# The first stage of a one-core encoder kernel: other queues, another order of loads and units

## The chip, the core and the metric

The kernel runs on one NeuronCore of a Trainium2 chip. The time is the device time of one execution in microseconds (us), as a median of several; less is better. Beside TensorE (PE, matrix products), VectorE (DVE), ScalarE (ACT) and GpSimd (POOL) there is SyncE (SP), which here only issues DMAs. Each engine works its own queue in order.

## The reference, cut to what matters

Two layers over `x` (1024 tokens, width 1024) and a memory of 256 tokens. What the change touches is the beginning: the norms of `mem` and `x`, and the first products that use them.

```python
def rmsnorm(x, g):
    y = x * rsqrt(mean(x * x, axis=-1) + EPS)
    return y * g

mem_n = rmsnorm(mem, mem_norm)                 # 256 x 1024
k, v = split(mem_n @ w_mem_kv[l], 2)           # for both layers l
h = rmsnorm(x, norm_even[0])                   # 1024 x 1024
qA, kA, vA, gA, qB, zBf, zBb, iB, gB, qM, gM = split_cols(h @ w_in_even[0], EVEN_SIZES)
...                                            # attention and gated scans, layer 2, final norm
```

## The kernel before, in words

All products are in float32 precision made from three passes. `split_w` rounds a loaded weight tile `raw` to a high part `hi` (ScalarE, two copies of 128x512) and computes the rest `lo` (VectorE, two subtractions); `mm3` then issues the three matmuls high x high, high x low, low x high (L195 to L197) for each of 8 slices of the inner dimension. Loads go through `load`, which issues them on SyncE in the order of the program; raw tiles `wr` have 2 buffers, `hi` (`wh`) and `lo` (`wl`) have 3 each, PSUM tiles of products (`mm`) 2, of transposes (`so`) 2.

`norm_T` normalizes up to four tiles of 128 tokens and turns them: squares with row sums on ScalarE (L254), the inverse root on VectorE in nine tiny steps (`rsqrt`, L137 to L152), the scaling on VectorE (L258), then for each of 8 slices the transposes on TensorE (L262), the product with the norm's weights and rounding on ScalarE (L266, the high half) and the low half on VectorE (L267). The norm's weights are columns of `vec`, which `vectors()` makes: seven small loads into `vrow`, 16 warm-up matmuls on the identity (L81), one transpose (L83) and a copy to `vec` (L84).

The stage starts with `mem_norm_T`. Then `start` hands out units: products of the memory with `w_mem_kv` (four with K columns, `proj_fm`, and two with V columns, `proj_tm`, for layer 0), the loads of the two halves of `x` (`x_load`), the norms of these halves, and the value product `v` of the first pair of B heads (columns O_IB of `w_in_even`, eight tiles of 128 tokens, copied out by VectorE at L871). `constants()` computes masks (L105 to L118), the lower bound `lbt` (L92 to L98, with one Exp on ScalarE at L94) and the sink factors `sks` (L127, from the small load `skr`). `weave` runs a unit's load one unit ahead of its work.

The order on each engine is not that of the program: a scheduler that works at compile time takes instructions by priority and by its own estimate of when they are ready. Instructions under `tc.high_priority()` go first; loads under `keep_in_program_order` keep their order. What it decided can be read from the built program, engine by engine.

Of the kernel before, what the change touches and what calls it, by code (L numbers as in the profile page):

```python
# [13 lines left out]
ALU = mybir.AluOpType  # L14
# [10 lines left out]
WARM = 16  # L25
MASK = -1e30
# [11 lines left out]
def tile_kernel(ctx, tc, x, mem, norm_even, w_in_even, sink, lb_param, hgrn_norm, w_out_even,  # L38
# [34 lines left out]
    def vectors():  # L73
        vrow = st([NV, P], "t2")
        for off, src, n in ((V_MN, mem_norm, 8), (V_NE, norm_even[0], 8), (V_NO, norm_odd[0], 8),
                            (V_HN, hgrn_norm[0], 4), (V_GN, gla_norm[0], 8)):
            load(vrow[off:off + n, :], src.rearrange("(a p) -> a p", p=P))
        load(vrow[V_LB:V_LB + 8, :], lb_param[0].rearrange("d (a p) -> (d a) p", p=P))
        load(vrow[V_BG:V_BG + 8, :], b_gate[0].rearrange("d (a p) -> (d a) p", p=P))
# [80 lines left out]

    def split_w(raw, hi, lo):

        k = raw.shape[1] // 2
        for i in range(2):
            ks = slice(i * k, i * k + k)
            nc.scalar.copy(hi[:, ks], raw[:, ks])  # L166
            nc.vector.tensor_tensor(lo[:, ks], raw[:, ks], f32(hi[:, ks]), ALU.subtract)  # L167
# [13 lines left out]
    def load_tm(w, c0, n=256):  # L181

        r = []
        for kh in range(2):
            raw = st([P, KT // 2, n], "wr")
            load(raw, w[kh * 512:kh * 512 + 512, c0:c0 + n].rearrange("(k p) c -> p k c", p=P))
            hi, lo = st([P, KT // 2, n], "wh", F32R), st([P, KT // 2, n], "wl", F32R)
            split_w(raw, hi, lo)
            r.append((hi, lo))
        return r  # L190
# [36 lines left out]
    def proj_tm(w, c0, hT, cb, n=256, nt=NT):  # L227
# [13 lines left out]
        yield Unit(lambda: box.append(load_tm(w, c0, n)), lambda: run(0))  # L241
# [3 lines left out]
    def norm_T(tiles, gv, hh, hl):  # L245
# [9 lines left out]
        with tc.high_priority():  # L255
            y = rsqrt(ss[:, :n], n, 1.0 / D)
            for i, xt in enumerate(tiles):
                nc.vector.tensor_scalar(xn[i], xt, y[:, i:i + 1], None, ALU.mult)  # L258
        for k in range(KT):
# [5 lines left out]
            with tc.high_priority():  # L265
                nc.scalar.activation(hh[:, k, :], pv, AF.Identity, scale=g)  # L266
                nc.vector.scalar_tensor_tensor(hl[:, k, :], pv, g, f32(hh[:, k, :]), ALU.mult, ALU.subtract)  # L267
# [465 lines left out]
    def x_load():  # L733
# [64 lines left out]
    kv = chain(mem_kv(0, mT), mem_kv(1, mT))  # L798

    def start(v):  # L800
# [3 lines left out]

        yield from some(2)
# [62 lines left out]
    def even_main():  # L868
        for pair in range(2):
            Vt = st([P, NT, 256], "t8")  # L870
            v = proj_tm(W0, O_IB + 256 * pair, hT, lambda t, ps, Vt=Vt: nc.vector.tensor_copy(Vt[:, t, :], ps))  # L871
# [275 lines left out]
```

## Time and profile before

| | before |
|---|---|
| median of 3 runs | 1489.28 us (1489.16 to 1489.79) |
| profiled execution, its own time | 1488.72 us |
| its span in the trace | 1486.9 us |
| TensorE busy | 1455.1 us (98% of the span) |
| VectorE, ScalarE, GpSimd busy | 885.0, 679.6, 33.8 us |
| mean granted TensorE clock | 0.994 of full speed |

The span runs from the first to the last recorded instruction; the profiled execution lasted 1.8 us longer. Times below are us from the span's start. An engine's wait is shown in square brackets behind the instruction that ended it: how long it sat idle, and who released it. "x4" is a count of merged instructions. [...]

### The profile page before, as it was taken

What the parts mean: (1) busy time and instruction counts of PE and PEld (TensorE: products, weight loads), DVE (VectorE), ACT (ScalarE), POOL (GpSimd) and SP (SyncE); (2) the same over time, 40 slices, a digit from 0 to 9 for tenths busy, and PEclk for the clock granted to TensorE, in tenths of its full rate; (3) what the DMA queues carried; (4) which work ended last, traced back from release to release, by engine and by line L of the source; (5) the groups of instructions that cost most, each with busy time, mean ns of one, the idle gap of its engine ahead of it and who ended that gap; (6) DMA issues with size and microseconds to landing.
All of it is one profiled execution on the core that took longest, in us unless ns stands there. A gap on an engine that the chain in (4) does not pass through costs nothing.

```text
span 1486.9 us, 27605 instructions
## 1 busy us (share of the span) xinstructions
PE 1455.1 (98%) x11337; PEld 1209.0 (81%) x11337; DVE 885.0 (60%) x2112; ACT 679.6 (46%) x1497; POOL 33.8 (2%) x75
## 2 busy tenths in 40 slices
PE   7999999999999999999999999999999999999997
PEld 7888898889776777888788797979788888878885
DVE  6536767675786474535376458585653456652577
ACT  6434333443476465435246455454346433641353
POOL 0000000000000000000000000000001000000000
PEclk9999999999999999999999999999999999999998
DMA  7424111011100213111264111101113221101622
GB/s 226 158 85 145 56 30 44 30 30 44 34 25 36 71 43 121 43 29 29 92 240 142 43 46 28 33 26 34 40 41 123 79 87 43 30 15 43 238 88 100
DMA packets 104231, 107.39 MB, mean 72 GB/s; under 512 B 13012, under 2 KB 85768, under 8 KB 103592
## 3 DMA queue, kind: packets, MB, share of 16 engines
q1 hardware_dynamic: 97848, 86.15, 18.6%
q0 software_dynamic: 5104, 17.37, 3.0%
q8 instruction: 89, 1.46, 0.4%
q10 hardware_dynamic: 1152, 2.10, 0.4%
q14 instruction: 38, 0.31, 0.1%
HBM read 84.64 MB, written 20.97 MB: 71 GB/s over the span
## 4 chain that ended last, share of the span: by engine, by line
PE 84%; DVE 8%; ACT 6%; issue 1%; DMA 1%; SPq 0%; ACTq 0%
PE pmm L196 21%; PE pmm L195 21%; PE pmm L197 21%; PE pso L413 4%; DVE big L342 3%; ACT s L308 2%; PE pso L579 2%; PE plv L377 1%; PE pat L574 1%; PE plv L398 1%; DVE wl L167 1%; ACT wh L166 1%; PE pat L335 1%; PE pat L500 1%; PE pat L361 1%
## 5 line engine op out<-in xcount | busy, mean ns | idle before, releaser
L195 PE MATMUL pmm<-hT,wh 128*128 128x512 f32 x896 | 355.4, 397 | 1.6 <-ACT wh L166 1.5
L196 PE MATMUL pmm<-hT,wh 128*128 128x512 f32 x896 | 354.5, 396 | 0.0
L197 PE MATMUL pmm<-hT,wl 128*128 128x512 f32 x896 | 353.3, 394 | 0.0
L167 DVE TENSOR_TENSOR wl<-wr,wh 128x512 fp32r<-128x512 f32 x188 | 127.2, 688 | 183.9 <-ACT wh L166 173.4
L166 ACT CAST wh<-wr 128x512 fp32r<-128x512 f32 x188 | 113.6, 620 | 258.0 <-PE pmm L196 167.6
L195 PEld LDWEIGHTS pmm<-hT,wh 128*128 128x128 f32 x896 | 168.3, 188 | 36.0 <-ACT wh L166 2.2
L197 PEld LDWEIGHTS pmm<-hT,wl 128*128 128x128 f32 x896 | 168.3, 188 | 34.8 <-issue 0.8
L196 PEld LDWEIGHTS pmm<-hT,wh 128*128 128x128 f32 x896 | 168.4, 188 | 33.3 <-issue 0.4
L195 PE MATMUL pmm<-wh,hT 128*128 128x256 f32 x448 | 128.5, 287 | 0.0
L197 PE MATMUL pmm<-wh,hT 128*128 128x256 f32 x448 | 127.4, 284 | 0.0
L196 PE MATMUL pmm<-wl,hT 128*128 128x256 f32 x448 | 127.3, 284 | 0.0
L602 DVE TENSOR_TENSOR ms<-big,ms 128x256 fp32r<-128x256 f32 x192 | 80.4, 422 | 62.5 <-ACT ms L601 59.7
L601 ACT CAST ms<-big 128x256 fp32r<-128x256 f32 x192 | 77.3, 406 | 85.8 <-PE pmm L197 72.1
L196 PE MATMUL pmm<-hT,ms 128*128 128x512 f32 x256 | 100.4, 392 | 0.4 <-DVE hT L167 0.4
L195 PE MATMUL pmm<-hT,ms 128*128 128x512 f32 x256 | 100.1, 391 | 0.0
L197 PE MATMUL pmm<-hT,ms 128*128 128x512 f32 x256 | 99.9, 390 | 0.0
L195 PEld LDWEIGHTS pmm<-wh,hT 128*128 128x128 f32 x448 | 86.3, 193 | 0.1
L196 PEld LDWEIGHTS pmm<-wl,hT 128*128 128x128 f32 x448 | 86.3, 193 | 0.1
L197 PEld LDWEIGHTS pmm<-wh,hT 128*128 128x128 f32 x448 | 86.3, 193 | 0.0
L308 ACT COPY s<-big 128x1024 f32<-128x1024 f32 x40 | 47.1, 1177 | 66.8 <-DVE big L342 63.1
L749 DVE TENSOR_TENSOR big<-big,t 128x512 f32<-128x512 f32 x48 | 33.0, 689 | 71.1 <-ACT t L747 71.0
L342 DVE TENSOR_TENSOR big<-big,tsm 128x512 f32<-128x512 f32 x96 | 61.1, 688 | 14.1 <-ACT s L308 7.0
(257 smaller groups left out, 2588.0 us busy)
## 6 DMA issues: line engine op xcount, KB each, us to landing
wr<-in_w_in_even_dram SPq DMA_DIRECT2D x34, 512.0 KB, 3.5
wr<-in_w_in_odd_dram SPq DMA_DIRECT2D x32, 512.0 KB, 4.1
wr<-in_w_mem_kv_dram SPq DMA_DIRECT2D x16, 512.0 KB, 5.3
x<-xi POOLq DMA_DIRECT2D x32, 256.0 KB, 2.3
t<-x SPq DMA_DIRECT2D x16, 512.0 KB, 4.9
wr<-in_w_out_odd_dram SPq DMA_DIRECT2D x12, 512.0 KB, 4.4
kv<-s POOLq DMA_DIRECT2D x8, 512.0 KB, 4.4
i<-in_x_dram SPq DMA_DIRECT2D x8, 512.0 KB, 7.7
```

Of the source, the lines that this page charges most:

```text
L166: nc.scalar.copy(hi[:, ks], raw[:, ks])
L167: nc.vector.tensor_tensor(lo[:, ks], raw[:, ks], f32(hi[:, ks]), ALU.subtract)
L195: nc.tensor.matmul(ps, ah, bh, start=(i == 0), stop=False)
L196: nc.tensor.matmul(ps, ah, bl, start=False, stop=False)
L197: nc.tensor.matmul(ps, al, bh, start=False, stop=(i == last))
L308: nc.scalar.copy(kh.rearrange("p (b h j) -> p b h j", h=2, j=m), sub(Xa, 0, [[2 * m, nb], [3 * N + m, 2], [1, m]]))
L342: nc.vector.tensor_tensor(xv, xv, tv, ALU.mult)
L413: nc.tensor.matmul(po[:, :dv], a, b, start=(j == 0), stop=(j == len(ops) - 1))
L579: nc.tensor.matmul(po[64 * i:64 * i + 64, :], va[:, b0 + b - 1, ks], PT[b - 1][:, 256 * i:256 * i + 256], start=(b == 1), stop=(b == nb))
L601: nc.scalar.copy(ms[:, 0], src)
L602: nc.vector.tensor_tensor(ms[:, 1], src, f32(ms[:, 0]), ALU.subtract)
L749: nc.vector.tensor_tensor(ds, ds, tmp, ALU.mult)
```

## The change

Five things, all in the first 80 us of the program:

- `vectors()` is called before the loads of `mem`; its seven small loads go to GpSimd's queue; `vec` is copied by ScalarE with high priority; five more identity matmuls (`KEEP`) stand behind the transpose.
- The first weight's rounding is queued behind that copy and behind the scaling of `mem` (`issue_after` keeps an instruction behind a named one of the same engine), the second's behind the fourth slice of the mem norm.
- `x` comes in quarters of two tiles, and the units that load them stand earlier.
- The value weights of the first pair are loaded early in four quarters into tiles that are idle there (`ms`, `xi`), and rounded from these (new lines L198 and L199).
- The two V products of the memory no longer stand between the loads and norms of `x`: both norms and the value product come before them.

```diff
@@ vectors()
-            load(vrow[off:off + n, :], src.rearrange("(a p) -> a p", p=P))
+            nc.gpsimd.dma_start(vrow[off:off + n, :], src.rearrange("(a p) -> a p", p=P))
...
         nc.tensor.transpose(vps, vrow, ident[:NV, :NV])
-        nc.vector.tensor_copy(vec, vps)
+        with tc.high_priority():
+            behind.append(nc.scalar.copy(vec, vps).ins)
+        for _ in range(KEEP):
+            nc.tensor.matmul(pt("mm")[:, :P], ident, ident, start=True, stop=True)
@@ split_w
+        with ExitStack() as order:
+            for i in behind.pop(0) if behind else ():
+                order.enter_context(tc.issue_after(i))
+            for i in range(2):
...
@@ load_tm(w, c0, n=256, raws=None)
+            if raws:
+                for i in range(2):
+                    ks = slice(2 * i, 2 * i + 2)
+                    nc.scalar.copy(hi[:, ks], raws[2 * kh + i])
+                    nc.vector.tensor_tensor(lo[:, ks], raws[2 * kh + i], f32(hi[:, ks]), ALU.subtract)
@@ mem_norm_T
+        vectors()
         tiles = []
...
-        vectors()
         mT = st([P, 2, KT, NMEM], "big", F32R)
-        norm_T(tiles, V_MN, mT[:, 0], mT[:, 1])
+        scaled, moved = norm_T(tiles, V_MN, mT[:, 0], mT[:, 1])
+        behind.append([behind.pop(), scaled])
+        behind.append(moved[3])
@@ x_load
-            if t % 4 == 3:
-                yield tiles[t - 3:]
+            if t % 4 % 2 == 1:
+                yield tiles[t - t % 4:]
@@ load_early (new)
+        for i in range(4):
+            raw = st([P, 2, 256], "ms" if i < 3 else "xi")
+            load(raw, W0[256 * i:256 * i + 256, O_IB:O_IB + 256].rearrange("(k p) c -> p k c", p=P))
+            yield raw
@@ start
         yield from some(2)
-        yield then(lambda: xh.append(next(xl)))
-        yield from some(2)
-        yield then(lambda: norm_T(xh[0], V_NE, *hT[0]))
+        yield x_part()
         yield from some(1)
-        yield then(lambda: xh.append(next(xl)))
+        yield x_part()
+        yield from some(1)
+        yield Unit(lambda: raws.extend(load_early()), lambda: None)
+        yield x_part()
+        yield x_part()
+        yield then(lambda: norm_T(xh[1], V_NE, *hT[0]))
         yield next(v)
-        yield then(lambda: norm_T(xh[1], V_NE, *hT[1]))
-        yield from some(1)
+        yield then(lambda: norm_T(xh[3], V_NE, *hT[1]))
         yield then(constants)
```

The order that the scheduler makes of it is shown at three places. In names, `t` in a norm is the scaled tile, `pso` the PSUM tile of a transpose, `pmm` that of a product, `big_149` and `big_159` the normalized memory, `hT` the normalized x. A line of the changed kernel is 9 to 33 higher than the same line before.

ScalarE, from the second square of `mem` on, before:

```order
L254 ACTIVATE t_38_151,sm_150<-i_16_102 128x1024
L254 ACTIVATE t_38_151,sm_150<-i_17_104 128x1024
L166 CAST wh_221<-wr_219 128x512 x2
L166 CAST wh_229<-wr_227 128x512 x2
L266 ACTIVATE big_149<-pso_166,vec 128x256
L266 ACTIVATE big_149<-pso_171,vec 128x256
L94 ACTIVATE lbt<-lbt 128x8
```

and in the changed kernel:

```order
L269 ACTIVATE t_43_161,sm_160<-i_39_155 128x1024
L269 ACTIVATE t_43_161,sm_160<-i_40_157 128x1024
L86 COPY vec<-pso_142 128x52
L175 CAST wh_231<-wr_229 128x512 x2
L98 ACTIVATE lbt<-lbt 128x8
L282 ACTIVATE big_159<-pso_176,vec 128x256
L282 ACTIVATE big_159<-pso_181,vec 128x256
L282 ACTIVATE big_159<-pso_186,vec 128x256
```

The copy of `vec` is now here and the first rounding behind it; the Exp of `lbt` (L94, now L98) has moved ahead of the first high half (L266, now L282), and the second weight's rounding behind the first high halves.

VectorE, ahead of the first low half of the memory, before:

```order
L167 TENSOR_TENSOR wl_222<-wr_219,wh_221 128x512 x2
L114 TENSOR_TENSOR mask_78<-mask_78,mi 128x32
L127 TENSOR_SCALAR sks<-skr 128x1 x2
L167 TENSOR_TENSOR wl_230<-wr_227,wh_229 128x512 x2
L84 COPY vec<-pso_146 128x52
L92 TENSOR_TENSOR lbt<-vec 128x8
L93 TENSOR_TENSOR lbt<-vec,lbt 128x8
L267 SCALAR_TENSOR_TENSOR big_149<-pso_166,vec,big_149 128x256
```

and in the changed kernel, from the last mask on:

```order
L118 TENSOR_TENSOR mask_78<-mask_78,mi 128x32
L131 TENSOR_SCALAR sks<-skr 128x1 x5
L96 TENSOR_TENSOR lbt<-vec 128x8
L131 TENSOR_SCALAR sks<-skr 128x1 x2
L97 TENSOR_TENSOR lbt<-vec,lbt 128x8
L131 TENSOR_SCALAR sks<-skr 128x1
L176 TENSOR_TENSOR wl_232<-wr_229,wh_231 128x512 x2
L283 SCALAR_TENSOR_TENSOR big_159<-pso_176,vec,big_159 128x256
L283 SCALAR_TENSOR_TENSOR big_159<-pso_181,vec,big_159 128x256
```

Between the scaling of `mem` and these rows stand 14 more mask instructions, which before stood partly between the steps of `rsqrt`. One weight's low part (L167, now L176) instead of two stands ahead of the first low half, and the copy of `vec` is gone.

TensorE, where the transposes of the second half of `x` begin, before:

```order
L196 MATMUL pmm_613<-wl_522,hT_83 128x256
L197 MATMUL pmm_613<-wh_521,hT_84 128x256
L262 MATMUL pso_676<-ident,t_111_656 128x128
L262 MATMUL pso_683<-ident,t_111_656 128x128
L262 MATMUL pso_676<-ident,t_111_656 128x128
L262 MATMUL pso_683<-ident,t_111_656 128x128
L195 MATMUL pmm_732<-wh_641,big_149 128x256
L196 MATMUL pmm_732<-wl_642,big_149 128x256
L197 MATMUL pmm_732<-wh_641,big_149 128x256
L195 MATMUL pmm_732<-wh_641,big_149 128x256
```

and in the changed kernel:

```order
L211 MATMUL pmm_557<-wl_397,hT_83 128x256
L212 MATMUL pmm_557<-wh_396,hT_84 128x256
L278 MATMUL pso_604<-ident,t_104_584 128x128
L278 MATMUL pso_611<-ident,t_104_584 128x128
L278 MATMUL pso_604<-ident,t_104_584 128x128
L278 MATMUL pso_611<-ident,t_104_584 128x128
L278 MATMUL pso_604<-ident,t_105_587 128x128
L278 MATMUL pso_611<-ident,t_105_587 128x128
L278 MATMUL pso_604<-ident,t_105_587 128x128
L278 MATMUL pso_611<-ident,t_105_587 128x128
L210 MATMUL pmm_717<-wh_390,hT_85 128x256
L211 MATMUL pmm_717<-wl_391,hT_85 128x256
```

Before, the V products of the memory (`pmm_732`) stand between the transposes; now the eight first transposes follow each other directly behind the fourth value tile (`pmm_557`), and the next products need the result of these transposes. The transposes of the first half read alike: between them stood `pmm_457`, and now nothing stands there.

## Rows read from the trace of the kernel before

**Rows 1.** Timeline, VectorE, first 24 us: start, duration, engine, line, operation, count, wait.

```profile
6.86 0.17 DVE L137 TENSOR_SCALAR sm<-sm 128x2 f32<-128x2 f32 x1 [6.86 <-ACT t L254]
...
8.80 1.41 DVE L258 TENSOR_SCALAR t<-i,sm 128x1024 f32<-128x1024 f32 x2
...
10.31 0.15 DVE L127 TENSOR_SCALAR sks<-skr 128x1 f32<-128x1 f32 x1
10.38 0.17 DVE L112 TENSOR_SCALAR mi<-mi 128x32 int32<-128x32 int32 x1
...
10.59 0.19 DVE L114 TENSOR_TENSOR mask<-mask,mi 128x32 int32<-128x32 int32 x1
...
12.40 1.28 DVE L167 TENSOR_TENSOR wl<-wr,wh 128x512 fp32r<-128x512 f32 x2
13.60 0.21 DVE L84 COPY vec<-pso 128x52 f32<-128x52 f32 x1
...
14.41 0.48 DVE L267 SCALAR_TENSOR_TENSOR big<-pso,vec,big 128x256 fp32r<-128x256 f32 x1 [0.21 <-ACT big L266]
...
21.56 0.88 DVE L267 SCALAR_TENSOR_TENSOR big<-pso,vec,big 128x256 fp32r<-128x256 f32 x2 [0.92 <-ACT big L266]
```

**Rows 2.** Timeline, ScalarE, 13 to 25 us.

```profile
13.90 0.47 ACT L266 ACTIVATE big<-pso,vec 128x256 fp32r<-128x256 f32 x1 [1.97 <-DVE vec L84]
...
23.38 1.06 ACT L254 ACTIVATE t<-big 128x1024 f32<-128x1024 f32 x1
```

**Rows 3.** Timeline, TensorE, start of the third product with the memory.

```profile
24.00 0.38 PE L195 MATMUL pmm<-big,wh 128*128 128x256 f32 x1 [0.45 <-DVE s L457]
```

**Rows 4.** Timeline, VectorE, scaling of the first half of x.

```profile
28.88 2.07 DVE L258 TENSOR_SCALAR t<-big,sm 128x1024 f32<-128x1024 f32 x3
...
31.20 0.74 DVE L258 TENSOR_SCALAR t<-big,sm 128x1024 f32<-128x1024 f32 x1
```

**Rows 5.** Chain of waits, 24 to 43 us: start, duration, what.

```profile
33.17 6.73 DMA wr<-in_w_in_even_dram
```

**Rows 6.** Timeline, ScalarE, rounding of the first layer's value weights.

```profile
40.00 0.62 ACT L166 CAST wh<-wr 128x512 fp32r<-128x512 f32 x1 [3.88 <-DMA wr<-in_w_in_even_dram]
```

**Rows 7.** Timeline, TensorE, last matmul before the gap, transposes behind it.

```profile
38.86 0.28 PE L197 MATMUL pmm<-wh,hT 128*128 128x256 f32 x1
42.06 1.10 PE L262 MATMUL pso<-ident,t 128*128 128x128 f32 x4 [2.92 <-DVE hT L267]
```

**Rows 8.** Windows: busy us and instructions by engine, PEclk, DMA share, GB/s.

```profile
11.00:11.50 0.50, 0.00 (x0) 0.00 (x0) 0.50 (x2) 0.50 (x2) 0.00 (x0) 0.90 0.00 0
...
42.00:42.50 0.50, 0.44 (x2) 0.44 (x3) 0.17 (x2) 0.50 (x2) 0.00 (x0) 0.62 1.08 412
45.50:46.00 0.50, 0.50 (x6) 0.50 (x5) 0.46 (x1) 0.50 (x1) 0.00 (x0) 0.97 1.00 324
```

**Rows 9.** Timeline, ScalarE, high halves of the second half of x.

```profile
57.88 1.27 ACT L266 ACTIVATE hT<-pso,vec 128x512 fp32r<-128x512 f32 x2 [7.51 <-PE pso L262]
...
66.03 0.69 ACT L266 ACTIVATE hT<-pso,vec 128x512 fp32r<-128x512 f32 x1 [0.26 <-PE pso L262]
```

**Rows 10.** Timeline, TensorE, end of the value product.

```profile
77.82 0.28 PE L197 MATMUL pmm<-wh,hT 128*128 128x256 f32 x1
77.94 0.28 PE L195 MATMUL pmm<-big,wh 128*128 128x256 f32 x1
```

**Rows 11.** Timeline, GpSimd, DMA issues.

```profile
31.57 0.54 POOL L469 DMA_DIRECT2D kv<-s  x1 [0.30 <-DVE s L457]
...
777.03 0.99 POOL L976 DMA_DIRECT2D wr<-in_w_gate_up_dram  x2 [0.29 <-POOL wr L974]
```

**Rows 12.** DMA issues by kind: count, KB each, us to landing.

```profile
wr<-in_w_gate_up_dram POOLq DMA_DIRECT2D x2, 32.0 KB, 1.9
skr<-in_sink_dram POOLq DMA_DIRECT2D x1, 4.0 KB, 4.5
```

**Rows 13.** Window of 200 us, columns as in rows 8.

```profile
350.00:550.00 200.00, 194.47 (x1496) 149.14 (x1495) 130.23 (x376) 114.25 (x289) 10.97 (x20) 1.00 0.13 43
```

More of the change, by code (lines that the diff above doesn't have):

```diff
@@ L25 @@
 WARM = 16
+KEEP = 5
 MASK = -1e30
@@ L76, in vectors @@
                             (V_HN, hgrn_norm[0], 4), (V_GN, gla_norm[0], 8)):
-            load(vrow[off:off + n, :], src.rearrange("(a p) -> a p", p=P))
-        load(vrow[V_LB:V_LB + 8, :], lb_param[0].rearrange("d (a p) -> (d a) p", p=P))
-        load(vrow[V_BG:V_BG + 8, :], b_gate[0].rearrange("d (a p) -> (d a) p", p=P))
+            nc.gpsimd.dma_start(vrow[off:off + n, :], src.rearrange("(a p) -> a p", p=P))
+        nc.gpsimd.dma_start(vrow[V_LB:V_LB + 8, :], lb_param[0].rearrange("d (a p) -> (d a) p", p=P))
+        nc.gpsimd.dma_start(vrow[V_BG:V_BG + 8, :], b_gate[0].rearrange("d (a p) -> (d a) p", p=P))
         for _ in range(WARM):
@@ L159, in half @@
         return slice(th * 512, th * 512 + 512)
+    behind = []
     def split_w(raw, hi, lo):
         k = raw.shape[1] // 2
[L164 to L167, printed above, removed]
+        with ExitStack() as order:
+            for i in behind.pop(0) if behind else ():
+                order.enter_context(tc.issue_after(i))
+            for i in range(2):
+                ks = slice(i * k, i * k + k)
+                nc.scalar.copy(hi[:, ks], raw[:, ks])
+                nc.vector.tensor_tensor(lo[:, ks], raw[:, ks], f32(hi[:, ks]), ALU.subtract)
     def load_fm(w, cols):
@@ L179, in load_fm, with load_tm @@
         return hi, lo, n
-    def load_tm(w, c0, n=256):
+    def load_tm(w, c0, n=256, raws=None):
         r = []
         for kh in range(2):
-            raw = st([P, KT // 2, n], "wr")
-            load(raw, w[kh * 512:kh * 512 + 512, c0:c0 + n].rearrange("(k p) c -> p k c", p=P))
             hi, lo = st([P, KT // 2, n], "wh", F32R), st([P, KT // 2, n], "wl", F32R)
-            split_w(raw, hi, lo)
+            if raws:
[3 more added lines that the diff above has]
+                    nc.vector.tensor_tensor(lo[:, ks], raws[2 * kh + i], f32(hi[:, ks]), ALU.subtract)
+            else:
+                raw = st([P, KT // 2, n], "wr")
+                load(raw, w[kh * 512:kh * 512 + 512, c0:c0 + n].rearrange("(k p) c -> p k c", p=P))
+                split_w(raw, hi, lo)
             r.append((hi, lo))
@@ L240, in run @@
                     cb(t, ps)
-        yield Unit(lambda: box.append(load_tm(w, c0, n)), lambda: run(0))
+        yield Unit(lambda: box.append(load_tm(w, c0, n, raws)), lambda: run(0))
         if nt > 4:
@@ L257, in norm_T @@
             for i, xt in enumerate(tiles):
-                nc.vector.tensor_scalar(xn[i], xt, y[:, i:i + 1], None, ALU.mult)
+                scaled = nc.vector.tensor_scalar(xn[i], xt, y[:, i:i + 1], None, ALU.mult)
+        done = []
         for k in range(KT):
@@ L265, in norm_T @@
             with tc.high_priority():
-                nc.scalar.activation(hh[:, k, :], pv, AF.Identity, scale=g)
-                nc.vector.scalar_tensor_tensor(hl[:, k, :], pv, g, f32(hh[:, k, :]), ALU.mult, ALU.subtract)
+                a = nc.scalar.activation(hh[:, k, :], pv, AF.Identity, scale=g)
+                d = nc.vector.scalar_tensor_tensor(hl[:, k, :], pv, g, f32(hh[:, k, :]), ALU.mult, ALU.subtract)
+                done.append((a.ins, d.ins))
+        return scaled.ins, done
     def new_hT(l):
@@ L803, in some, with x_part @@
             return (next(kv) for _ in range(n))
+        def x_part():
+            return Unit(lambda: xh.append(next(xl)), lambda: None)
         yield from some(2)
-        yield then(lambda: xh.append(next(xl)))
-        yield from some(2)
-        yield then(lambda: norm_T(xh[0], V_NE, *hT[0]))
+        yield x_part()
         yield from some(1)
-        yield then(lambda: xh.append(next(xl)))
+        yield x_part()
[4 more added lines that the diff above has]
+        yield then(lambda: norm_T(xh[1], V_NE, *hT[0]))
         yield next(v)
-        yield then(lambda: norm_T(xh[1], V_NE, *hT[1]))
-        yield from some(1)
+        yield then(lambda: norm_T(xh[3], V_NE, *hT[1]))
         yield then(constants)
```

7 lines of the change are left out of this document (5 added, 2 removed).

## Prediction

> **What bounds the kernel now.** I read the page's busy times first, then windows, then the timeline of each engine up to 80 us and the chain of waits from 24 to 43. TensorE is busy for 98% of the span, and behind the first stage it hardly stops: the worst 200 us, from 350 to 550, leave it idle for 200 - 194.47 = 5.5 us [rows 13]. So the change has to win in the first stage. That stage ends at 77.94, where the eight value tiles are done and the next product begins [rows 10]. By the order TensorE has then run 384 matmuls of 256 columns and 80 transposes; two matmuls start 0.12 apart [rows 10] and a transpose takes about as long, so 464 x 0.12 = 55.7 us of work, and 22.2 us are lost. The reader should see three losses. The first high half of the mem norm starts at 13.90, released by the copy of `vec` [rows 2], which stands behind two pairs of weight roundings [rows 1]. TensorE idles 2.92 us until 42.06 [rows 7], because ScalarE waited 3.88 us for the value weights [rows 6], a load under way for 6.73 us [rows 5]. And TensorE's granted clock fell to its lower level (1.2 GHz) twice, near 11.45 and near 42.1, after stretches with nothing or a few transposes; the second time it was back at 45.5 [rows 8]. These 3.4 us at half speed cost 1.7 us of work.
>
> **The head.** GpSimd issues two small loads in 0.99 us [rows 11], so seven from about 1.0, with the identity between, end near 5, and land 1.9 to 4.5 us after their issue [rows 12]: `vec` is there between 7.6 (the end of the warm-up) and 9.5. That is far earlier than 13.60 [rows 1], but the next thing in line is late too. On ScalarE the Exp of `lbt` now stands ahead of the first high half, and it waits for VectorE, where 15 mask rows and the sink factors come first. The norm's inverse root ends as before; without masks between its steps the scaling ends at 10.1 instead of 8.80 + 1.41 = 10.2 [rows 1]. A row that needs its predecessor follows it after 0.21 (10.38 to 10.59), a free one after 0.07 (10.31 to 10.38) [rows 1]. Nine mask rows wait for VectorE itself by the order: 9 x 0.21 + 6 x 0.07 = 2.3, then five sink factors 0.35, then two steps of `lbt` 0.4: 13.1, the Exp 0.2: the first high half at 13.3, 0.6 earlier. Bounds: all 23 rows free, 11.7; all dependent, 14.9. VectorE still has one weight's low part ahead of the first low half, 1.28 [rows 1]: 13.1 + 1.3 = 14.4, against 14.41 [rows 1]. The third slice's transposes wait for that half (two buffers), so nothing is won there. Stepping through the other slices by these durations, with TensorE at its upper clock, the last low half ends at 21.7 instead of 21.56 + 0.88 = 22.4, and the third product starts at 23.45 instead of 24.00 [rows 3]: **-0.55** (0 if the clock falls here as before, -2 if the rows are all free). The five extra matmuls run in idle time, up to 9.7; only if `vec` came after 11.3 would the weight's rounding, and with it the stage, be later.
>
> **Fourth product.** Its weight's low part stands on VectorE behind seven steps of x's inverse root, which wait for the last square of x. Two copies of K results are now ahead of that square, so it ends at 25.05 instead of 23.38 + 1.06 + 0.2 = 24.6 [rows 2]; 25.05 + 7 x 0.2 + 0.7 = 27.15, and TensorE, ready at 26.45, idles **+0.7** (0 to 1.2). It ends at 29.8.
>
> **First half of x.** The scaling ends at 32.05, as before (31.20 + 0.74 [rows 4]), since VectorE was the bound already. But the V product of the memory, 48 matmuls or 5.8 us, lay beside it and now stands far behind. From 29.8 until the first high half is ready at 33.25 TensorE has eight transposes, 1.0 us: **+2.5** (1.5 to 3.2).
>
> **Value weights.** Their quarters need no `wr` buffer; they are issued at 19 to 20, right behind the fourth K weight, and wanted at 26.6. Even the slow load took 6.73 [rows 5], so they are there. The idle 2.92 and the slow clock behind it go: **-4.6** (2.92 + 1.7; -2.9 if that clock fall comes elsewhere). The loads of x's second half land around 31, ten us before use, which hides them; a delay beyond 41 would count in full.
>
> **Second half of x.** Each slice takes about 1.2: the last six of the old second half came at (66.03 - 58.5)/6 = 1.26, with weight roundings between [rows 9]. So the first two value tiles, woven with the slices, end at 42.2, the next two at 42.55 + 48 x 0.12 = 48.3. The four squares stand behind the last high half on ScalarE: 41.0 + 4 x 1.06 = 45.2. VectorE copies the third tile, takes nine steps (1.8), four scalings at 0.67 (2.07 for three [rows 4]) and a copy: 50.85, and the first high half is ready at 52.05. Before, three value tiles and a V product lay beside this chain; now only two value tiles, and TensorE idles from 48.3 to 52.05 less 1.0 of transposes: **+2.8** (2 to 3.5). Then eight slices (8.9), a buffer (0.35), 48 matmuls (5.8) and the 96 of the V products (11.5): 78.5 against 77.94.
>
> **The sum.** -0.55 + 0.7 + 2.5 - 4.6 + 2.8 = +0.85; the walk itself gives +0.6, the slices being less disturbed, and I take +0.6. It holds no clock fall. There are two new stretches like the old ones, 29.8 to 33.25 and 48.3 to 52.05, with transposes dotted in them as in the old head, where the clock fell all the same [rows 8]. A fall costs up to 1.7; part of that hides behind the chain of 1.2 per slice. I count one fall at 1.0 (bounds: none, or three at 1.7 or less). 1488.72 (the profiled execution's own time) + 1.6 = 1490.3; the median lies 0.56 above that execution, so **1490.9**. The stall goes from the weights to the two scalings of x: that is what is late next. Behind the stage the scheduler's order also differs, on TensorE up to a third of the program; I price that at 0, with bounds of -2.7 and +2.7, half of the idle time in [rows 13].
>
> **Rivals.** *The clock falls three times, slower:* in the head (0.6, as before) and in both new stretches (1.7 each). +0.6 + 4.0 = 4.6 over 1489.28: 1493.9. For it: all three stretches hold less work than the old ones that fell, or as little. Against it: the head's is shorter by five matmuls, and transposes are work. It decides from the second fall at full price on: 0.6 + 1.7 + 0.6 = 2.9, just the 0.2% below. Chance 0.15.
>
> *The small loads come late, slower:* they are seven issues in a row by software, and `skr`, which the sink factors need at about 12.7, is the eighth, issued at 5.4; it has 7 us where the worst took 4.5 [rows 12]. If it came at 15 the stage moves by 2.3: 1488.72 + 1.6 + 2.3 + 0.56 = 1493.2. Chance 0.05. [...]
>
> *The waits are shorter than I stepped them, faster:* VectorE's mask rows run freely (-1.4), no clock falls (-1.0), and the new order behind the stage closes half of the idle time of [rows 13] (-2.7): 1490.9 - 5.1 = 1485.8. Each is possible, and the stage has 22 us to give; against it, no engine's order shortens a chain behind 24 us. Chance 0.27.
>
> *It changes nothing that counts:* the gains of the head end in VectorE's queue and no clock falls: 1489.3, chance 0.03.
>
> **How the numbers follow.** My own forecast, 1488.5 to 1493, has a chance of 0.50. What this measurement can tell from no change is about 0.2%, 3 us. Of the forecast 0.44 lies within that and 0.06 above 1492.3; the late loads and three falls add 0.20 to slower, the faster rival 0.25 to faster and 0.02 to no change, the last 0.03 to no change: faster 0.25, no change 0.49, slower 0.26. The range leaves out about the far third of both sides: 1485.2 to 1494.0.
>
> **What would show it.** In the changed kernel: `vec` copied near 8, but the first high half not before 13, released by VectorE; TensorE idle near 27, from 30 to 33 and from 48 to 52, and not near 40; no wait of ScalarE for the value weights; the V products of the memory at their end near 78.5; the clock at 0.5 at most behind one of the new stretches. The prediction is wrong if the first high half starts near 10.6, or if TensorE finds work in these two stretches, which the order does not show.

## The result: 0.5% slower

The changed kernel takes 1497.1 us (median of 4 runs, 1496.6 to 1498.48), the kernel before 1489.53 in the same session (4 runs, 1489.16 to 1490.23): a ratio of 1.0053, 95% interval 1.0041 to 1.0065, so some 7.6 us slower. The forecast was 1490.9 with a range up to 1494.0. The profiled execution took 1496.6 us, its span is 1494.8.

The page of the changed kernel, first lines:

```profile
span 1494.8 us, 27643 instructions
...
PE 1461.1 (98%) x11347; PEld 1211.6 (81%) x11347; DVE 889.8 (60%) x2111; ACT 680.0 (45%) x1498; POOL 37.4 (3%) x82
```

98% busy as before says nothing; the places do. ScalarE's timeline, in the head and at the second half of x:

```profile
9.84 0.20 ACT L86 COPY vec<-pso 128x52 f32<-128x52 f32 x1 [2.98 <-PE pso L84]
...
13.11 0.82 ACT L282 ACTIVATE big<-pso,vec 128x256 fp32r<-128x256 f32 x2
...
52.46 1.27 ACT L282 ACTIVATE hT<-pso,vec 128x512 fp32r<-128x512 f32 x2 [6.46 <-PE pso L278]
```

`vec` is there 3.8 us earlier than in [rows 1] and the first high half 0.8 us earlier than in [rows 2]. TensorE's timeline, start of the third product, and of the first product behind all that the stage of before did:

```profile
24.22 0.39 PE L210 MATMUL pmm<-big,wh 128*128 128x256 f32 x1 [0.45 <-DVE s L477]
...
81.09 0.40 PE L210 MATMUL pmm<-hT,wh 128*128 128x512 f32 x1
```

The 0.8 us of the head have gone by the third product: 24.00 in [rows 3]. The memory's value products now end the stage, at 81.09 us, against 77.94 in [rows 10]: 3.15 us later. Windows (length, then busy us of TensorE, weight loads, VectorE, ScalarE and GpSimd with their instructions, granted clock, DMA share, GB/s):

```profile
28.00:32.00 4.00, 3.62 (x28) 3.26 (x28) 4.00 (x10) 2.21 (x5) 0.25 (x1) 1.00 1.03 397
32.00:36.00 4.00, 2.70 (x20) 2.02 (x19) 3.94 (x7) 1.83 (x3) 0.82 (x2) 1.00 0.99 384
...
48.00:52.00 4.00, 2.88 (x20) 1.99 (x18) 3.82 (x10) 0.00 (x0) 0.00 (x0) 1.00 0.00 0
52.00:56.00 4.00, 3.19 (x16) 2.75 (x17) 1.59 (x4) 1.95 (x3) 0.00 (x0) 0.73 0.00 0
56.00:60.00 4.00, 4.00 (x30) 3.93 (x29) 2.35 (x4) 2.06 (x3) 0.00 (x0) 0.85 0.00 0
...
130.00:135.00 5.00, 2.52 (x79) 2.21 (x77) 2.56 (x4) 2.99 (x5) 0.00 (x0) 1.00 0.77 214
...
140.00:145.00 5.00, 4.16 (x143) 3.14 (x143) 4.93 (x11) 2.83 (x5) 1.05 (x2) 1.00 0.12 48
...
150.00:155.00 5.00, 4.21 (x80) 3.25 (x78) 3.91 (x8) 2.57 (x4) 0.00 (x0) 1.00 0.57 175
```

The two gaps of the forecast are there, near 32 to 36 us and 48 to 54 us, with a clock fall behind the second, and next to none near 40. What I did not forecast is the last block: 4.1 us without work from 130 to 155 us. The kernel before lacks 0.7 us there:

```profile
135.00:140.00 5.00, 4.76 (x62) 3.62 (x49) 5.00 (x9) 2.39 (x5) 1.06 (x2) 1.00 0.54 213
140.00:145.00 5.00, 4.52 (x81) 3.83 (x82) 4.86 (x11) 2.08 (x3) 0.00 (x0) 1.00 0.35 105
```

The list of waits of the changed kernel for 125 to 160 us (engine, line, tile, releaser: us in total, times, longest):

```profile
ACT wh L175 <- DMA wr<-in_w_in_even_dram: 3.9, 1, 3.9
...
DVE s L887 <- DMA kv<-s: 3.2, 1, 3.2
...
PE plv L313 <- DVE s L887: 2.5, 1, 2.5
```

`s` is a tag of four buffers (s4). The memory's keys and values of layer 1 fill all four until they are stored, and the first scan's first product (L887, then L313 on TensorE) wants one. The issue of the keys' store on GpSimd, after:

```profile
126.58 0.53 POOL L488 DMA_DIRECT2D kv<-s  x1 [43.57 <-ACT s L476]
```

and before:

```profile
112.53 0.53 POOL L468 DMA_DIRECT2D kv<-s  x1 [43.86 <-ACT s L456]
```

It is 14 us later, against a scan whose first product runs at about the same time (132.44 us after, 132.69 before). The reason is a count of units. The two value products of layer 0's memory left the first stage and joined the list that `among` deals out two at a time behind the heads' units, so that everything behind them on this list moved by two places against the unit that starts the scan. The last x tile that layer 0 stores is a mark that both kernels share. GpSimd's timeline has it before at

```profile
565.23 0.55 POOL L630 DMA_DIRECT2D x<-xi  x1 [12.04 <-ACT xi L629]
```

and after at

```profile
573.52 0.55 POOL L650 DMA_DIRECT2D x<-xi  x1 [12.04 <-ACT xi L649]
```

From the end of the first stage to this mark it is 487.3 us before and 492.4 after. So of the 8.3 us that the mark is late, 3.15 are of the first stage and 5.1 of what lies between. Nothing is lost behind the mark (the end is 7.9 us later).

### The profile page after: what moved, and what is told of

It is laid out like the page before. It is cut to its first block, busy times and chain, and to the rows that moved or that the text cites. A ratio compares the mean times of both kernels' runs of the same rounds, so it can differ in the third digit from the quotient of the medians.

```text
span 1494.8 us, 27643 instructions
## 1 busy us (share of the span) xinstructions
PE 1461.1 (98%) x11347; PEld 1211.6 (81%) x11347; DVE 889.8 (60%) x2111; ACT 680.0 (45%) x1498; POOL 37.4 (3%) x82
## 4 chain that ended last, share of the span: by engine, by line
PE 80%; issue 9%; ACT 5%; DVE 4%; DMA 1%; POOL 1%; ACTq 0%; POOLq 0%
PE pmm L211 20%; PE pmm L210 20%; PE pmm L212 20%; PE pso L431 4%; PE pso L599 2%; PE plv L395 1%; PE pat L594 1%; DVE big L360 1%; PE plv L416 1%; ACT s L326 1%; PE plv L340 1%; PE pat L353 1%; PE pat L520 1%; PE pat L379 1%; PE plv L570 1%
## 5 line engine op out<-in xcount | busy, mean ns | idle before, releaser
L176 DVE TENSOR_TENSOR wl<-wr,wh 128x512 fp32r<-128x512 f32 x184 | 124.0, 688 | 168.8 <-ACT wh L175 141.4
```

## The experiments

My first theory (theory 1) was that the order of units is the whole loss, in two parts, the unfilled gaps and the store; the rival (theory 2) put it in the head and the clock. All times are medians; "before" in the same sessions was 1489.05 to 1489.52 us.

**The value products back between the norms, nothing else changed.**

```
+        yield from some(1)
         yield then(lambda: norm_T(xh[1], V_NE, *hT[0]))
+        yield from some(1)
         yield next(v)
```

> The changed kernel with one edit: the two value products of the first layer's memory stand again between the norms, one ahead of the first half of x, one ahead of the second, as in the kernel before. Theory 1 (two losses by the order alone): in the changed kernel TensorE lacks this work in the gaps at 30 to 34 and 48 to 54 us (3.4 us less busy there, and a clock fall at 54 to 57 us of some 1.7 us), and, as the memory's products of layer 1 end two places later in the order of units, the store of that layer's keys (126.58 us) holds the s4 buffers that the first scan wants, so that VectorE's L887 waits 3.2 us and TensorE 2.5 us at 131 to 134 us, with 4.5 us lost up to 225 us. With the edit both go: the wait of L887 for kv is under 0.5 us, and the time is 1487.0 to 1490.0 us. Theory 2 (the loss is the head's rounding behind the norm and the clock falls in the head, and the stall at 131 us only moves): the time stays over 1494 us.

Measured: 1493.9 us, ratio to before 1.0028 (1.0016 to 1.0039). Neither number. The store is at 116.86 us and the scan waits for none; but the first gap grew to 3.2 us without work from 28 to 40 us (1.7 in the changed kernel), and the clock fell at its end (0.53 over 36 to 40 us, 0.62 over 40 to 44). TensorE's timeline:

```profile
33.68 1.31 PE L278 MATMUL pso<-ident,t 128*128 128x128 f32 x8 [1.46 <-DVE hT L283]
35.90 1.77 PE L278 MATMUL pso<-ident,t 128*128 128x128 f32 x8 [0.91 <-DVE hT L283]
...
39.09 0.78 PE L210 MATMUL pmm<-wh,big 128*128 128x256 f32 x2
```

The filler begins at 39.09, behind the transposes that it should lie between: its weights are queued on SyncE from 24.77 on, behind the value weights and the second half of x, and the schedule puts it late. A gap with a filler is only as good as the filler's weights.

**The value products behind the second norm.**

```
         yield then(lambda: norm_T(xh[3], V_NE, *hT[1]))
+        yield from some(2)
         yield then(constants)
```

> The changed kernel with one edit: the two value products of the first layer's memory stand right behind the second norm instead of among the products of the first heads. TensorE's gaps at 30 to 34 and 48 to 54 us then stay as they are, and only the place of the memory's products of layer 1 in the order is that of the kernel before. Theory 1: the keys' store moves from 126.6 us to some 113 to 117 us, the first scan's L887 no longer waits for it, the 4.5 us behind the stage come back and no more: 1491.5 to 1493.5 us. Theory 2 (the later loss has to do with the order in which weights are loaded on SyncE's queue, or with the store not at all): 1496 to 1498 us with a wait of similar size at the first scan.

Measured: 1491.9 us, ratio 1.0014 (1.0005 to 1.0023): inside theory 1's range, 5.2 us gained. But the first stage did not stay as it was, which the expectation took for granted. The first gap did, yet behind the second scaling of x TensorE is busier and the clock does not fall:

```profile
48.00:52.00 4.00, 4.00 (x36) 3.94 (x36) 3.51 (x8) 0.00 (x0) 0.00 (x0) 1.00 0.00 0
52.00:56.00 4.00, 3.38 (x28) 3.01 (x27) 3.19 (x6) 3.58 (x6) 0.00 (x0) 1.00 0.00 0
```

The stage ends at 79.40 us instead of 81.09, so 1.7 us of the gain lie there. The rest lies behind it: to the last x tile it is 487.7 us, 492.4 in the changed kernel. GpSimd's timeline has the keys' store nearly back at its old time, and of the windows at the scan only one lacks more than a trace of work:

```profile
113.98 0.53 POOL L488 DMA_DIRECT2D kv<-s  x1 [44.19 <-ACT s L476]
```

```profile
140.00:145.00 5.00, 4.31 (x81) 3.32 (x79) 4.89 (x10) 1.77 (x2) 0.00 (x0) 1.00 0.40 127
```

**Before, with the early value weights alone** (raws and their rounding as in the diff; loaded behind the fourth key weights).

```
         yield from some(2)
+        yield Unit(lambda: raws.extend(load_early()), lambda: None)
         yield then(lambda: norm_T(xh[0], V_NE, *hT[0]))
```

> The kernel before with one part of the change: the first layer's value weights are loaded early, behind the fourth key weights of the memory, into idle tiles. Theory 1: each part of the change by itself is sound and only the order of the memory's value products costs; the gap of 2.9 us at 39 to 42 us and the clock fall behind it (granted 0.53 and 0.62 over 42 to 46 us) go, so 1484.5 to 1487.0 us. Theory 3 (the early loads delay the memory's value weights or x by as much as they save): 1488.5 to 1490.5 us, with a new wait for DMA between 24 and 36 us.

Measured: 1485.0 us, ratio 0.9965 (0.9953 to 0.9978): faster than both kernels, the best of this study. The windows show the gap of [rows 7] and the clock fall of [rows 8] gone:

```profile
36.00:40.00 4.00, 4.00 (x36) 3.92 (x36) 3.89 (x7) 3.92 (x8) 0.00 (x0) 1.00 1.03 358
40.00:44.00 4.00, 4.00 (x36) 4.00 (x35) 3.53 (x7) 2.68 (x6) 0.00 (x0) 1.00 0.57 197
44.00:48.00 4.00, 4.00 (x35) 4.00 (x35) 1.25 (x6) 2.81 (x6) 0.00 (x0) 1.00 0.46 131
```

**Before, with the new head alone** (small loads, copy of `vec`, five warm products, rounding queued).

> The kernel before with the head of the change alone: small loads first and on GpSimd's queue, the vectors copied by ScalarE, five warm products behind the transpose, rounding of weights queued behind the norm of the memory. By my terms the third product is 0.55 us earlier and the fourth waits 0.7 us: the stage ends about 0.15 us later, 1489.0 to 1490.5 us. Theory 2 (the head is what costs): 1492.5 us or more, with the fourth product's wait or a clock fall larger than in the kernel before.

Measured: 1488.6 us, ratio 0.9993 (0.9984 to 1.0002): no change that can be told, so theory 2 has fallen.

**The whole change but the order of the memory's products**, with x's second half queued behind their first weights.

```
-        yield x_part()
-        yield x_part()
         yield then(lambda: norm_T(xh[1], V_NE, *hT[0]))
+        yield from some(1)
+        yield x_part()
+        yield x_part()
         yield next(v)
         yield then(lambda: norm_T(xh[3], V_NE, *hT[1]))
+        yield from some(1)
```

> The changed kernel with the memory's two value products in the places of the kernel before, as in the first experiment, and besides the loads of the second half of x queued on SyncE behind the weights of the first of these products. In the first experiment those weights stood behind 3 MB (value weights and second half of x); the rounding ScalarE waited up to 2.9 us for them, TensorE stood at that product with x's transposes behind it, and it was busy 1.64 of 32 to 36 us. Theory 1 (the moved products and the loads queued ahead of them are the whole loss): this wait goes, the first scan waits for no store, and with the rest of the change kept the time is 1483.5 to 1486.0 us. Theory 2 (something else of the change costs too, the quarters of x or the head): 1488 us or more.

(This expectation reads the first experiment wrongly in one detail: the 2.9 us are a wait for other, later weights. In the first stage the longest such wait is 1.4 us; what stood there is the order shown above.) Measured: 1487.0 us, ratio 0.9987 (0.9978 to 0.9996), 1 us above the range of theory 1. The order is worth 10.1 us, all of the loss and more, yet 2 us are missing against the early weights alone.

**Before, with the order of the memory's products alone.**

```
-        yield from some(1)
         yield then(lambda: xh.append(next(xl)))
         yield next(v)
         yield then(lambda: norm_T(xh[1], V_NE, *hT[1]))
-        yield from some(1)
```

> The kernel before with one part of the change alone: the memory's two value products leave the first stage for places among the first heads' products. Theory 1 (the order alone costs, whatever else is changed): the store of layer 1's keys is late at the first scan here too, L854 waits 2 to 4 us for it, 4.5 to 5.2 us, and the first stage's gaps lose their filler, 1 to 4 us: 1494.5 to 1499.0 us. Theory 3 (the products cost only where they also lose the early value weights or meet the changed order of loads): 1488.5 to 1491.0 us.

Measured: 1502.0 us, ratio 1.0087 (1.0073 to 1.0101): above the range of theory 1, and worse than the changed kernel, where the early weights can pay some of it back. The waits at the scan are the same two (L852 2.8 us for the store, ScalarE 4.9 us for weights).

**The changed kernel with layer 1's keys in idle tiles**, which leaves two of the four s4 buffers to the scan.

```
+        kk = [[st([P, 512], tag, F32R) for tag in tags] for tags in (("ms", "ms"), ("ms", "xi"))] if l else None
...
+            if i == 0 and l:
+                h, c = c.start // 512, slice(c.start % 512, c.start % 512 + NMEM)
+                th, tl = kk[0][h], kk[1][h]
...
```

> The changed kernel in its own order of units, with one edit: the keys of the memory's layer 1 are kept in four idle tiles of half the size (ms and xi) and stored from there in four pieces, so that two of the four s4 buffers are free when the first scan begins. Theory 1 (the scan waits for the s4 buffers that the store holds, and for nothing else): L887's wait for the store is gone, TensorE's gap at 131 to 134 us too, and the time falls by the 4.5 to 5.2 us that moving the products gave: 1491.5 to 1493.0 us. Theory 4 (the gain of the second experiment came from its other order of products and weights, not from the store): the gap stays in size with another releaser, 1495.5 to 1498 us.

Measured: 1498.0 us, ratio 1.0054 (1.004 to 1.0067). Theory 1 has fallen in its second part. The wait did go: VectorE's timeline has the scan's first product 3.5 us earlier, waiting for nothing:

```profile
128.92 1.22 DVE L898 TENSOR_TENSOR s<-big 128x1024 f32<-128x1024 f32 x1
```

but the windows give as much back:

```profile
135.00:140.00 5.00, 3.65 (x88) 3.41 (x88) 4.88 (x10) 2.62 (x5) 0.00 (x0) 1.00 0.06 19
...
150.00:155.00 5.00, 2.90 (x72) 2.21 (x71) 4.19 (x7) 1.82 (x3) 0.00 (x0) 0.87 0.08 17
155.00:160.00 5.00, 5.00 (x79) 3.66 (x78) 2.87 (x7) 1.25 (x3) 0.00 (x0) 0.79 0.28 92
```

3.45 us without work and a slow clock, against 4.1 in the changed kernel; in both gaps TensorE waits for an operand of the scan from ScalarE (1.35 and 2.10 us). From the end of the stage (80.87) to the last x tile (573.41) it is 492.5 us, as in the changed kernel (492.4). The changed kernel's list of waits names a want of buffers (L887 for the store, 3.2 us, once), and this run shows that it was not the price.

**The new head and the early weights, x in halves, old order.**

> The kernel before with two parts of the change, the new head and the early value weights behind the fourth key weights; order of units and x in halves as before. If the parts add up, 1485.0 us of the early weights less 0.9 us of the head: 1483.5 to 1485.0 us. If the head's gain was noise or is taken back behind it: 1485.0 to 1486.5 us.

Measured: 1487.3 us, ratio 0.9988 (0.9979 to 0.9997), above both ranges: the parts don't add up, the head takes 2.3 us back. ScalarE's timeline:

```profile
25.66 1.06 ACT L269 ACTIVATE t<-big 128x1024 f32<-128x1024 f32 x1 [1.14 <-DMA big<-in_x_dram]
...
27.03 0.62 ACT L175 CAST wh<-wr 128x512 fp32r<-128x512 f32 x1 [0.21 <-DVE sm L141]
```

The fourth key weights are rounded at 27.03 us behind a square that waits for x; with the old head this is at 24.46. SyncE's issues say why x is late:

```profile
14.28 0.37 SPq L160 DMA_DIRECT2D wr<-in_w_mem_kv_dram  x1
14.69 2.00 SPq L160 DMA_DIRECT2D big<-in_x_dram  x4
```

with the old head they go at 12.31 and 12.73. The third key weights wait for a `wr` buffer, the buffer for the rounding, and the rounding now waits behind the norm.

**The same without the queueing of the rounding.**

```
-        behind.append([behind.pop(), scaled])
-        behind.append(moved[3])
+        behind.clear()
```

> The kernel of the eighth experiment (new head and early value weights) without the queueing of the weights' rounding behind the memory's norm; small loads on GpSimd, the vectors' copy on ScalarE and the five warm products stay. In the eighth, VectorE's low halves of the first key weights run at 12.97 us, behind the norm's scaling, so that their wr buffer comes free later: SyncE's third key weights go at some 14.3 us, x right behind at 14.69 us (12.73 us with the old head), x's squares end 2.5 us later and the fourth key weights go at 18.44 instead of 14.89 us. Theory 5 (the queueing costs by the loads that it delays): without it the loads go at the old times and the time is 1483.0 to 1485.5 us. Theory 6 (the 2.2 us between the eighth and the third experiment are of another part of the head): 1486.5 to 1488.0 us.

Measured: 1487.9 us, ratio 0.9992 (0.9983 to 1.0001). Theory 5 has fallen: x's loads do go early (10.54 us), but then the norm's scaling stands behind four low parts of weights on VectorE, and the copy of `vec` behind one on ScalarE that waits 2.92 us for weights:

```profile
13.70 1.14 ACT L175 CAST wh<-wr 128x512 fp32r<-128x512 f32 x2 [2.92 <-DMA wr<-in_w_mem_kv_dram]
14.74 0.20 ACT L86 COPY vec<-pso 128x52 f32<-128x52 f32 x1
...
16.22 0.82 ACT L282 ACTIVATE big<-pso,vec 128x256 fp32r<-128x256 f32 x2
```

The first high half is 3.1 us later than in the changed kernel. Either the loads or the norm come late; the queueing trades one for the other.

**The changed kernel, three memory units behind each head unit.**

```
-            yield from among(chain(v, *hs), kv, 2)
+            yield from among(chain(v, *hs), kv, 3)
```

> The changed kernel with three instead of two of the memory's units behind each unit of the first heads, so that all of the memory's products end before the first scan begins; its first stage is untouched. In the seventh experiment the store no longer held the scan up (L898 waited for nothing) and the time did not fall: the gaps came 5 to 20 us later. Theory 7 (the scan's steps are VectorE's, and what runs on TensorE between them has to be the heads' products of 512 columns; the memory's value products of half the work leave it idle): as these end before the scan here, the later loss goes: 1491.5 to 1493.5 us. Theory 8 (the memory's late weights or the early stage bring the gaps whatever stands beside the scan): 1495 us or more.

Measured: 1494.8 us, ratio 1.0035 (1.0023 to 1.0048): between the theories. The gaps at the scan are small (0.6 us at 140 to 145), but half of the gain is missing: layer 0's last x tile is stored at 570.09 us, 3.4 us earlier than in the changed kernel, 0.6 of it from the first stage (80.51), and by the end 2.3 us are left. Where the rest is I did not find.

**The third experiment with layer 1's value products behind the scan's start.**

```
-            yield from among(chain(v, *hs), kv, 2)
+            yield from among(chain(v, *hs), kv, [2, 2, 1, 0, 2, 1] if pair == 0 else [])
```

(`among` is changed to take such a list of counts.)

> The kernel of the third experiment (before with early value weights, 1485.0 us) with one edit: the value products of the memory's layer 1 stand behind the unit that starts the first scan instead of ahead of it; the keys' products and so their store stay as early as there, and the first stage is untouched. Theory 7 (what costs is that these short products stand beside the scan's first steps): the gaps of the changed kernel at 130 to 160 us appear here, with no wait of the scan's first product for the store, and the time is 1488.0 to 1490.5 us. Theory 1 (only the keys' store counts): 1484.5 to 1486.0 us.

Measured: 1491.3 us, ratio 1.0014 (1.0005 to 1.0022), 6.3 us slower than the third experiment: theory 7, with a larger price, and no wait for the store on the list. From the end of the stage to the last x tile it is 494.4 us, 487.2 in the third experiment. TensorE's timeline shows the mechanism:

```profile
126.54 0.28 PE L203 MATMUL pmm<-wh,big 128*128 128x256 f32 x1
130.01 1.08 PE L328 MATMUL plv<-big,s 128*32 128x32 f32 x64 [3.19 <-ACT s L314]
131.07 0.58 PE L201 MATMUL pmm<-wh,big 128*128 128x256 f32 x1
```

The memory's product (256 columns), which was dealt between two of the scan's steps, has run out, and TensorE, in order, stands 3.19 us before the scan's 64 small products until VectorE and ScalarE have made their operand. Then the clock is at its lower level (granted 0.50 over 130 to 135 us), and the next matmul takes 0.58 us instead of 0.28.

**The whole change but the order, without the queueing.**

> The kernel of the fifth experiment (the change with the memory's products in their old places, 1487.0 us) without the queueing of the rounding behind the norm. Theory 5: the wr buffers come free earlier, the gaps of 0.4 to 0.6 us per 4 us at 20 to 32 us shrink: 1484.0 to 1486.0 us. Theory 6: 1486.5 to 1487.5 us.

Measured: 1489.1 us, ratio 0.9999 (0.999 to 1.0008): above both ranges, theory 5 has fallen here too.

**The changed kernel, layer 1's products dealt ahead of the scan's start, first stage untouched.**

```
-            yield from among(chain(v, *hs), kv, 2)
+            yield from among(chain(v, *hs), kv, [2, 2, 3, 2] if pair == 0 else [])
```

> The changed kernel with its first stage as it is; behind it the memory's units follow the first heads' units by 2, 2, 3 and 2 instead of by 2 each time, so that layer 1's value products stand directly ahead of the unit that starts the first scan, as in the kernel before. Theory 7 (only their place against the scan's start counts, as too short fillers beside its first steps or through the store behind them): the later loss of 5.2 us goes and that of the first stage stays: 1491.0 to 1493.5 us. Theory 9 (the weights that the shifted order loads late are the loss): 1494.5 us or more, with waits of ScalarE for weights of 2 us or more between 100 and 160 us.

Measured: 1492.3 us, ratio 1.002 (1.001 to 1.003): theory 7, and theory 9 has fallen, although ScalarE still waits up to 2.4 us for weights there. The first stage ends no earlier (81.71 us), and GpSimd stores layer 0's last x tile 5.5 us earlier than in the changed kernel, 486.3 us behind the stage's end instead of 492.4:

```profile
568.00 0.55 POOL L650 DMA_DIRECT2D x<-xi  x1 [12.04 <-ACT xi L649]
```

**The third experiment with eight idle products in the head.**

```
+            if n == 2 and k == 1:
+                for _ in range(8):
+                    nc.tensor.matmul(pt("mm")[:, :P], ident, xn[1][:, :P], start=True, stop=True)
```

> The kernel of the third experiment (1485.0 us) with eight idle products of 128 columns, whose results nothing reads, between the memory's first transposes and its first product, where TensorE waits from 10.7 to 14.5 us. If the clock's fall there (granted 0.5 from 12 to some 17 us) counts in full: no fall in the head, 1483.0 to 1484.0 us. If it hides behind the chain of roundings per slice, as I took it for a part: 1484.3 to 1485.5 us.

Measured: 1490.3 us, ratio 1.0005 (0.9996 to 1.0014): above both ranges, 5.3 us slower than the third experiment. It tells nothing on the clock's price. The clock fell all the same (0.50 over 12 to 16 us): half of the idle products (the x8 rows) were scheduled behind a transpose that waits for `vec`, and then stood ahead of the first real product. And the schedule behind changed too: TensorE lacks 2.7 us of work from 40 to 48 us, where the third experiment lacks none.

```profile
13.92 0.69 PE L268 MATMUL pso<-ident,t 128*128 128x128 f32 x2 [2.27 <-DVE vec L84]
14.40 1.91 PE L271 MATMUL pmm<-t,ident 128*128 128x128 f32 x8
```

**The changed kernel with nine idle products ahead of the second half's transposes.**

```
+        if tiles is xh_[0]:
+            for _ in range(9):
+                nc.tensor.matmul(pt("mm")[:, :P], ident, tiles[0][:, :P], start=True, stop=True)
```

(`xh_[0]` names the tiles of the second half.)

> The changed kernel with nine idle products of 128 columns, whose results nothing reads, ahead of the transposes of x's second half, where TensorE waits from 50 to 53 us and the clock then falls to 0.5 until 57.4 us. If that fall costs its full 1.7 us: the clock stays up and 1495.0 to 1496.0 us. If the slices' chain hides it: 1496.5 to 1497.5 us.

Measured: 1496.8 us, ratio 1.0053 (1.004 to 1.0065). The fall behind 54 us is gone, and so is the head's, without an edit there; another stands behind the first half of x instead:

```profile
32.00:36.00 4.00, 3.29 (x18) 2.88 (x17) 3.58 (x6) 1.95 (x3) 0.00 (x0) 0.75 1.03 396
...
52.00:56.00 4.00, 3.39 (x27) 2.92 (x26) 1.77 (x3) 1.91 (x3) 0.00 (x0) 1.00 0.00 0
```

So the time of the whole says nothing on a single fall. The timelines do, since the head and the second half of x here run the same code as in the changed kernel at the upper clock. ScalarE's first high halves of the memory and of x's second half, and TensorE's third product and first product behind the stage:

```profile
13.32 0.82 ACT L287 ACTIVATE big<-pso,vec 128x256 fp32r<-128x256 f32 x2
...
53.13 1.26 ACT L287 ACTIVATE hT<-pso,vec 128x512 fp32r<-128x512 f32 x2 [6.81 <-PE pso L283]
```

```profile
23.28 0.39 PE L210 MATMUL pmm<-big,wh 128*128 128x256 f32 x1 [0.60 <-DVE s L482]
...
80.43 0.40 PE L210 MATMUL pmm<-hT,wh 128*128 128x512 f32 x1
```

In the head it is 9.96 us from the one to the other, in the changed kernel 11.11 (13.11 to 24.22): the fall there cost 1.15 us. From x's second half to the end of the stage it is 27.30 us, in the changed kernel 28.63 (52.46 to 81.09): 1.3 us.

## Why the prediction was wrong

The runs give a chain from the changed kernel back to before, one edit at a time: layer 1's products at their old place against the scan -5.2 (1497.1 to 1491.9; by the profiled executions 1.7 of it in the first stage), filler back in the first stage with its weights in time -4.9 (to 1487.0), old head and x in halves -2.0 (to 1485.0), value weights late again +4.5 (to 1489.5). Each step is uncertain by some 2 us.

- **Value weights, -4.6.** Right: 4.5 us, idle time and clock fall together, as the sum had it. The lower level reads in the trace of before as granted 0.50 from 42.5 to 45.5 us, with matmuls of 256 columns 0.215 us apart (1.2 columns per ns) instead of 0.12; the third experiment has 1.00 from 36 to 48 us.
- **The head, -0.55, and the fourth product, +0.7.** The steps were right in kind: first high half 13.11 (forecast 13.3), released by VectorE's rows behind the masks; first low half 14.15 (14.4); last one's end 22.26 (21.7). But the clock fell in the head (0.57 over 16 to 20 us), so the third product started at 24.22, not 23.45, just beyond the bound that I had named for this (no gain against 24.00); without the fall it starts at 23.28, in the fifteenth experiment. The fourth product waited 0.56 us. `vec` was copied at 9.84, not near 8, with nothing waiting for it. Alone the head changes nothing measurable. That it costs some 2 us where the early weights have closed the other gap I missed. By the eighth's trace, I costed the rounding's wait on VectorE and not the `wr` buffer that it holds, for which SyncE's queue waits, with x behind. But undoing the queueing gained nothing (ninth, twelfth), so that this chain is the price is not shown.
- **First half of x, +2.5.** TensorE lacks 1.7 us of work from 28 to 36 us, within the bounds (1.5 to 3.2).
- **Second half of x, +2.8, and one clock fall, +1.0.** The first high half starts at 52.46, and TensorE's next product, which the forecast had at 52.05, at 53.20; the head's clock fall is worth as much. TensorE lacks 1.9 us of work from 48 to 56 us, a little under the bound of 2. The clock fell twice, in the head and behind 54 us, by the windows 1.7 us of work each ((1 - 0.57) x 4; (1 - 0.73) x 4 + (1 - 0.85) x 4). By the fifteenth experiment the two cost 1.15 and 1.3 us. Two falls at 2.5 us together instead of one at 1.0 make up the difference between +1.6 as forecast and the +3.15 measured at the stage's end; without them it would end at 78.6, and the walk gave 78.5. So the walk through the first stage held as a whole, and the clock's term in it was too small.
- **"Behind the stage the scheduler's order also differs [...]; I price that at 0."** This is the step that failed. It lost 4.75 us in the profiled execution (7.9 less the 3.15 of the stage), above the bound of 2.7. The thirteenth experiment, which puts back only this and leaves the first stage as late, gained 4.8 us. I saw that two products moved out of the stage and costed the hole that they left, but not the place where they arrived: ahead of layer 1's products, which so come two units later, beside a scan. I took the bound from the worst 200 us of before [rows 13], and idle time of before bounds what can be won there, not what can be lost.
- **The mechanism of this loss.** Shown: the order against the scan's start costs this much (second, eleventh and thirteenth experiment, by the stretch from the stage's end to the last x tile), and it does so without any wait for the store (seventh, eleventh). TensorE's longest wait there in the changed kernel, for VectorE and through it for the store, is a symptom: with it gone the time is the same. The longest wait on the list, ScalarE's 3.9 us for weights, is not the price either: waits of this kind are left in the thirteenth experiment, 4.2 us in two, and the loss is gone. Argued, from the eleventh's timeline and the seventh's windows: the heads' products of 512 columns (matmuls 0.23 us apart) are long enough to cover a step of the scan on VectorE, the memory's of 256 columns (0.12 us) are not. The tenth experiment gained only half of what this says, which stays open.
- **The rivals.** "The clock falls three times" named the nearest time (1493.9). Two of its three falls came, but they explain only the first stage; most of the loss has another cause. "The small loads come late" did not happen: the seven were issued by 5.44 us, and `vec` was copied at 9.84.

## What to carry to other kernels

When work is moved out of a stage, cost its new place as closely as the hole: in a loop that deals units by count, two extra units shift all that follow, and a short unit beside a long step of another engine can leave the in-order TensorE standing (3.19 us in the eleventh experiment). A long wait on the list need not be the price: take it away by itself before believing it. And an edit that only loads earlier into idle tiles was worth more alone (4.5 us) than with all that was built around it.

## What the hardware showed

In these runs the clock's falls were not fixed to a place in the program. The head of the changed kernel ran at 0.57 over 16 to 20 us, and the same head at 1.00 in the fifth and the fifteenth experiment, with no more before it (1.70 us of TensorE's work from 12 to 16 us where it fell, 1.49 in the fifteenth, where it did not). Further in it is the same: the changed kernel is at 0.73 over 52 to 56 us and at 1.00 over 32 to 36, the fifteenth experiment at 1.00 and at 0.75.

The two falls of the changed kernel did not cost all that the windows show: 1.7 us each by the granted clock, they moved what came behind them by 1.15 and 1.3 us.
